# A two-layer RG-LRU and latent-attention trunk on one core: inputs in load order, x and w_ada transposed, modulation by row sums, eight column tiles in the first products

## The chip, the cores and the metric

One core of a Trainium2 chip runs the whole program. A core has five engines that run side by side, each in its own order: TensorE (PE, matmuls; PEld are its weight loads), VectorE (DVE), ScalarE (ACT), GpSimd (POOL) and SyncE (SP), which here issues every transfer; 16 DMA engines move the data. The metric is the device time of one execution in microseconds, as the median of several. Laying out the inputs on the host, ahead of the launch, is not part of it.

## The reference

A residual stream x (512 tokens by 1024) goes through two layers. In each:

```python
mod = (c @ w_ada + b_ada)[:, None, :]                 # c: 1 x 1024, w_ada: 1024 x 6144
sh_m, sc_m, g_m, sh_f, sc_f, g_f = jnp.split(mod, 6, axis=-1)
h = rms_norm(x) * (1 + sc_m) + sh_m
proj = h @ w_in                                       # 1024 x 3520
x_lru, q_down, kv_down, k_rope, gate_a, gate_b = jnp.split(proj, IN_SPLIT_POINTS, axis=-1)
y_a = rg_lru(causal_depthwise_conv(x_lru, conv_w, conv_b), positions, ...)   # 1024 columns
y_b = mla(q_down, kv_down, k_rope, cos, sin, q_norm_g, kv_norm_g, w_uq, w_ukv)  # 256 + 128 + 64
y = jax.nn.sigmoid(gate_a) * y_a + jax.nn.sigmoid(gate_b) * y_b              # 1024 + 1024
x = x + g_m * (y @ w_out)
h = rms_norm(x) * (1 + sc_f) + sh_f
gate, up = jnp.split(h @ w_ffn_in, 2, axis=-1)        # 1024 x 5632
x = x + g_f * ((jax.nn.silu(gate) * up) @ w_ffn_out)  # 2816 x 1024
```

The end is `rms_norm(x, final_norm_g)`. All is float32.

## The kernel before

**Products.** x is held transposed: eight tiles `x[j]` of 128 channels by 512 tokens. Each float32 operand of a product is split into a high and a low part (`split`: ACT rounds the high part to fp32r, DVE subtracts), and a product of 128x128 weights with 128x512 activations is three matmuls (`mm3`): high by high, high by low, low by high. A 128-column tile of `w_in` therefore takes 8 x 3 = 24 matmuls. Its weights come by one transfer into a `raw` buffer of 128x1024 (3 of them), are split into `whi` and `wlo` (3 each) and multiplied into a PSUM bank (8 in all).

**The order of work** is a planner's. The code only records operations; `Recorder.order` then plays them through with estimated durations (`cost`), waits and free buffers, and each engine takes next what has the longest way to the end; PE keeps the order of the code. The words of `SCRIPT` give the code's order in the mixer: `x` conv input, `g` gates, `e` and `w` the recurrence, `r`, `p`, `q`, `s`, `t`, `v` attention, `a`, `b` output gates, `y` merge, `m` one step of background work. Where PE would wait before the first products end, it runs filler matmuls (`fill`, at most `FILL_MAX`).

**The start of layer 0**, to which most of the change belongs:

- x is loaded by tokens: eight `xtok` tiles, whose squares ACT sums (`junk`); PE transposes them by 32 matmuls with `ident`, ACT copies them into `x[j]`. `rsqrt` makes the scale of each token, PE spreads it over the partitions, and it is copied as `rst0` (`rst` in the rows).
- `first_mods` forms the shift and scale of the first norm for one or two tiles j at a time (`FIRST`), as `P`: 8 matmuls per tile and vector, with a block of `w_ada` as weights and the conditioning column spread over 64 columns as the moving side (`pt<-cols,wa`), or as `V`: DVE multiplies and adds eight blocks into `wacc`, and PE sums its partitions (`pt<-ones,wacc`).
- `first_products` then has for each j one column set: `w_first` loads rows j of six column pieces of `w_in` (two of x_lru, two of q_down, kv_down and k_rope), 704 columns in two transfers, and five `mm3` and one `mm2` (k_rope, high and low side by side) add to six banks, 17 matmuls. Eight sets complete the six pieces.

**Modulation vectors later on** (`mod_steps`, 10 of the 12): eight blocks of 128 rows of `w_ada` by 1024 columns are loaded as `graw` (2 buffers); DVE multiplies each by its part of c and adds it to `macc` in two halves of 512; a transposing reduction (`mred`), one matmul with `sel` and four small DVE operations bring the 1024 sums into an 8-column tile. They are the background work: three in the mixer of layer 0, one in the feed-forward part of layer 0 with the six of layer 1.

**Loads.** A tile of 128 columns is read from the row-major weights as 128 partitions x 8 pieces of 512 bytes. Gate weights, `w_uq` and `w_ukv` come in two or three transfers per tile, and small parameters as rows (`rows1`, `rows2`), which PE transposes into columns (`cols1`, `cols2`).

**Small norms** (`small_norm`): squares, sums, `rsqrt`, spreading and scaling of q_down and kv_down, all at one place in the code, right after the first products.

In the rows all operations have the line L525, where the planner issues them; tiles tell them apart.

Of the kernel before, what the change touches and what calls it, by code (L numbers as in the profile page):

```python
# [12 lines left out]
F32 = mybir.dt.float32  # L13
# [4 lines left out]
ALU = mybir.AluOpType  # L18
# [16 lines left out]
OFF_Q = 1024  # L35
OFF_KV = 1280
OFF_KR = 1408
OFF_GA = 1472
OFF_GB = 2496
# [5 lines left out]
C_SEL = 128  # L45
C_MASK = 256
C_FREQ = 768
C_END = 769

R_C = 0  # L50
R_BADA = 8
R_QG = 104
R_KVG = 108
# [4 lines left out]
R_AP = 112  # L58

# [14 lines left out]
GTAG = "graw"  # L74
# [41 lines left out]
DMA_ISSUE = 470.0  # L116
TABLE_LOAD = 1300.0
# [82 lines left out]
class Recorder:  # L200
# [117 lines left out]
    def order(self):  # L318
# [15 lines left out]
        for o in reversed(ops):  # L334
            d = o.dur if o.eng != "SP" else o.bytes / DMA_RATE + DMA_LAT
# [204 lines left out]
def trunk(  # L540
    ctx: ExitStack,
    tc: tile.TileContext,
    x_in, c_in, pos_in, w_ada, b_ada, w_in, conv_w, conv_b,
    lru_wa, lru_ba, lru_wx, lru_bx, lru_ap, qg, kvg,
    w_uq, w_ukv, w_out, w_fi, w_fo, fng, consts, out,
# [66 lines left out]
    def w_cols(src, nk=KD, on_g=False, raws=None):  # L612

        raw = raw_tile()
        DMA.dma_start(raw[:, : nk * P].rearrange("p (k c) -> p k c", c=P), src.rearrange("(k p) c -> p k c", p=P))
        hi, lo = hl_tiles()
        if on_g:
            G.tensor_scalar(hi[:, : nk * P], raw[:, : nk * P], 1.0, 1.0, ALU.mult, ALU.mult)
            V.tensor_tensor(lo[:, : nk * P], raw[:, : nk * P], f(hi[:, : nk * P]), ALU.subtract)
        else:  # L620
            split(hi[:, : nk * P], lo[:, : nk * P], raw[:, : nk * P])
# [4 lines left out]
    def w_krope(l):  # L626

        raw = raw_tile()
        DMA.dma_start(
            raw[:, :512].rearrange("p (k c) -> p k c", c=64),  # L630
            w_in[l, :, OFF_KR : OFF_KR + 64].rearrange("(k p) c -> p k c", p=P),
        )
# [7 lines left out]
    def w_first(l, j, keep):  # L640


        if keep:
            r0, r1 = unit("wf0")[:, :256], unit("wf1")[:, :448]
        else:
            raw = raw_tile()
            r0, r1 = raw[:, :256], raw[:, 256:704]
        js = slice(j * P, (j + 1) * P)
        DMA.dma_start(r0, w_in[l, js, :256])
        DMA.dma_start(r1, w_in[l, js, OFF_Q : OFF_GA])  # L650
        hi, lo = hl_tiles()
# [12 lines left out]
        return parts, hi[:, 640:768], cols + [r1[:, 384:448]]

    def w_lru(l, n0):

        raw = raw_tile()
        for i, src in enumerate((lru_wa, lru_wx)):
            DMA.dma_start(  # L670
                raw[:, i * 512 : (i + 1) * 512].rearrange("p (n c) -> p n c", c=P),
                src[l, n0 : n0 + 4].rearrange("n p c -> p n c"),
            )
        return split_halves(raw, "lw")

    def w_rope(l, g):

        raw = raw_tile()
        for k in range(2):
            DMA.dma_start(  # L680
                raw[:, k * 256 : (k + 1) * 256].rearrange("p (h e) -> p h e", h=4),
                w_uq[l, k * P : (k + 1) * P, 4 * g : 4 * g + 4, NOPE:],
            )
        hi, lo = unit("rwh", F32R), unit("rwl", F32R)
        for k in range(2):
            ks = slice(k * 256, (k + 1) * 256)
            src = raw[:, ks].rearrange("p (h f i) -> p f h i", h=4, f=2)
            dh = hi[:, ks].rearrange("p (f h i) -> p f h i", h=4, f=2)
            dl = lo[:, ks].rearrange("p (f h i) -> p f h i", h=4, f=2)
            A.activation(dh, src, AF.Copy)  # L690
            V.tensor_tensor(dl, src, f(dh), ALU.subtract)
        return hi, lo

    def w_pair(l, p2):

        raw = raw_tile()
        for k in range(2):
            DMA.dma_start(
                raw[:, k * 256 : (k + 1) * 256].rearrange("p (h e) -> p h e", h=2),
                w_uq[l, k * P : (k + 1) * P, 2 * p2 : 2 * p2 + 2, :NOPE],  # L700
            )
        DMA.dma_start(raw[:, 512:].rearrange("p (h e) -> p h e", h=2), w_ukv[l, :, 2 * p2 : 2 * p2 + 2, :])
# [4 lines left out]
    DMA.dma_start(ident, consts[:, :C_SEL])  # L707
    ct = const([P, C_END - C_SEL], "ct")
    sel = ct[:, :P]
    mask = ct[:, C_MASK - C_SEL : C_MASK - C_SEL + 512]  # L710
    freq = ct[:, C_FREQ - C_SEL : C_FREQ - C_SEL + 1]

    rows1, rows2 = unit("rows1"), unit("rows2")
    V.memset(rows1[:, :P], 0.0)
    for rows, r0, n, src in (
        (rows1, R_C, 8, c_in.rearrange("b (j p) -> (b j) p", p=P)),
        (rows1, R_BADA, 96, b_ada.rearrange("l (j p) -> (l j) p", p=P)),
        (rows1, R_QG, 4, qg.rearrange("l (j p) -> (l j) p", p=P)),
        (rows1, R_KVG, 2, kvg),
    ):  # L720
        DMA.dma_start(rows[r0 : r0 + n, :P], src)

    cols1 = const([P, P], "cols1")
    cols2 = const([P, P], "cols2")

    def to_columns(rows, cols):
        ps = psum("pt")
        T.transpose(ps[:, :P], rows[:, :P], ident)
        V.tensor_copy(cols, ps[:, :P])

    to_columns(rows1, cols1)

    ones = const([P, P], "ones")
    V.memset(ones, 1.0)
    epsc = const([P, 1], "epsc")
# [10 lines left out]

    def mod_steps(l, s):

        acc = rec.tile(cp, [P, D], F32, "macc", 1, nm("macc"))
        for k in range(KD):  # L750
            raw = rec.tile(wp, [P, 1024], F32, GTAG, NGRAW if GTAG == "graw" else NRAW, nm("graw"))
            DMA.dma_start(raw, w_ada[l, k * P : (k + 1) * P, s * D : (s + 1) * D])
            ck = cols1[:, R_C + k : R_C + k + 1]
            for h in range(2):
                hs = slice(h * 512, (h + 1) * 512)
                if k == 0:
                    V.tensor_scalar(acc[:, hs], raw[:, hs], ck, None, ALU.mult)
                else:
                    V.scalar_tensor_tensor(acc[:, hs], raw[:, hs], ck, acc[:, hs], ALU.mult, ALU.add)
            yield  # L760
        red = small(32, "mred", 2)
        V.tensor_reduce(red, acc.rearrange("p (b i) -> p b i", i=32), AX.X, ALU.add, apply_transpose=True)
        ps = psum("o")
        T.matmul(ps[:, :32], sel, red, start=True, stop=True)
        m = const([P, 8], f"mod{l}_{s}")
        pv = ps[:, :32].rearrange("p (m r) -> p r m", r=4)
# [914 lines left out]
```

## Time and profile before

| What | Value |
|---|---|
| Median of 3 runs | 1352.01 us (1350.59 to 1353.84) |
| The profiled execution's own time | 1354.54 us |
| Its span, first to last instruction | 1352.5 us |
| DVE, ACT, POOL busy | 987.6, 669.9, 193.4 us (73%, 50%, 14%) |
| Moved by DMA | 175.00 MB, mean 129 GB/s |
| Mean granted clock of TensorE | 0.991 |

The profiled execution is one run of its own, so its time differs a little from the median. Busy time of engines overlaps; a share of the span says how much of the time an engine had an instruction in work, and matmuls are pipelined, so PE's counts overlap among themselves. The granted clock is the share of TensorE's full 2.4 GHz that the throttle gave in a stretch. Times in views are from the span's start.

### The profile page before, as it was taken

The page shows a single profiled execution, that of the slowest core. Times are in us where ns is not written, and L with a number is a line of the kernel's source. Part 1 is how long each engine was busy: PE and PEld are TensorE (multiplying, and loading weights), DVE is VectorE, ACT ScalarE, POOL GpSimd, SP SyncE. Part 2 cuts the span into 40 slices and gives each one's busy share as a digit, 9 for nine tenths or more (in the row PEclk, how much of TensorE's full clock was granted, in tenths as well). Part 3 has the DMA queues.
Part 4 walks back from the last instruction along what each step waited for, and adds up shares of the span by engine and source line. Part 5 has one row for each costly group of instructions (what it writes and reads, how often), then busy time and mean ns, then how long its engine had stood idle before and what let it go on. Part 6 is the DMA issues. An engine that isn't in the chain of part 4 may idle for free.

```text
span 1352.5 us, 18566 instructions
## 1 busy us (share of the span) xinstructions
PE 1331.4 (98%) x6924; PEld 1142.3 (84%) x6924; DVE 987.6 (73%) x1716; ACT 669.9 (50%) x1060; POOL 193.4 (14%) x224
## 2 busy tenths in 40 slices
PE   7999999999999999999999999999999999999997
PEld 7887888888888888888887888888888999999986
DVE  4689799788866556566769976757677877777744
ACT  4386768544523222222346877965364444434422
POOL 0122254411200000000040233422310000000000
PEclk9899999999999999999999999999999999999999
DMA  9544345235655555655534324221333433343321
GB/s 289 176 135 125 106 131 162 94 106 159 192 181 182 185 190 173 205 176 184 186 86 117 102 71 117 66 75 47 94 100 104 119 90 91 104 113 108 98 77 63
DMA packets 251046, 175.00 MB, mean 129 GB/s; under 512 B 12510, under 2 KB 235084, under 8 KB 250956
## 3 DMA queue, kind: packets, MB, share of 16 engines
q1 hardware_dynamic: 250956, 173.82, 43.4%
q8 instruction: 54, 0.88, 0.3%
q14 instruction: 36, 0.29, 0.1%
HBM read 167.50 MB, written 2.10 MB: 125 GB/s over the span
## 4 chain that ended last, share of the span: by engine, by line
PE 87%; DVE 5%; POOL 2%; ACT 2%; DMA 1%; issue 1%; SPq 0%; ACTq 0%; DVEq 0%; POOLq 0%
PE mm L525 77%; PE s L525 4%; PE pt L525 3%; PE o L525 3%; POOL sc L525 1%; POOL w L525 1%; DVE macc L525 1%; DVE xc L525 1%; DVE wlo L525 0%; SPq L525 0%; DVE ri L525 0%; DMA graw<-in_w_ada_dram 0%; DVE xn L525 0%; DVE wacc L525 0%; DMA raw<-in_w_in_dram 0%
## 5 line engine op out<-in xcount | busy, mean ns | idle before, releaser
L525 ACT ACTIVATE whi<-raw 128x1024 fp32r<-128x1024 f32 (+2 forms) x194 | 199.4, 1028 | 417.5 <-PE mm L525 328.8
L525 DVE TENSOR_TENSOR wlo<-raw,whi 128x1024 fp32r<-128x1024 f32 (+2 forms) x193 | 232.3, 1204 | 106.8 <-ACT whi L525 102.7
L525 PE MATMUL mm<-hh,whi 128*128 128x512 f32 x408 | 161.6, 396 | 0.0
L525 PE MATMUL mm<-hl,whi 128*128 128x512 f32 x408 | 160.8, 394 | 0.0
L525 PE MATMUL mm<-hh,wlo 128*128 128x512 f32 x400 | 157.3, 394 | 0.3 <-DVE wlo L525 0.3
L525 PE MATMUL mm<-al,whi 128*128 128x512 f32 (+1 forms) x360 | 139.1, 386 | 0.0
L525 PE MATMUL mm<-ah,whi 128*128 128x512 f32 (+1 forms) x360 | 138.9, 386 | 0.0
L525 PE MATMUL mm<-ah,wlo 128*128 128x512 f32 (+1 forms) x360 | 138.6, 385 | 0.0
L525 PE MATMUL mm<-fh,whi 128*128 128x512 f32 x336 | 130.9, 390 | 0.0
L525 PE MATMUL mm<-fh,wlo 128*128 128x512 f32 x336 | 130.9, 390 | 0.0
L525 PE MATMUL mm<-fl,whi 128*128 128x512 f32 x336 | 130.0, 389 | 0.0
L525 DVE SCALAR_TENSOR_TENSOR macc<-graw,cols,macc 128x512 f32<-128x512 f32 x140 | 101.8, 767 | 17.8 <-DMA graw<-in_w_ada_dram 17.5
L525 PEld LDWEIGHTS mm<-hl,whi 128*128 128x128 f32 x408 | 77.4, 190 | 15.5 <-DVE hl L525 0.5
L525 PEld LDWEIGHTS mm<-hh,whi 128*128 128x128 f32 x408 | 77.3, 189 | 15.5 <-DVE whi L525 0.2
L525 PE MATMUL mm<-xql,wsh 128*128 128x256 f32 x320 | 90.4, 283 | 0.0
L525 PE MATMUL mm<-xqh,wsl 128*128 128x256 f32 x320 | 90.3, 283 | 0.0
L525 PE MATMUL mm<-xqh,wsh 128*128 128x256 f32 x320 | 90.2, 283 | 0.0
L525 PEld LDWEIGHTS mm<-hh,wlo 128*128 128x128 f32 x400 | 75.9, 190 | 16.5 <-DVE wlo L525 1.2
L525 ACT ACT_TABLE_LOAD x60 | 77.0, 1283 | 6.7 <-DVE mx L525 3.2
L525 PEld LDWEIGHTS mm<-ah,wlo 128*128 128x128 f32 x360 | 67.7, 188 | 13.1
L525 PEld LDWEIGHTS mm<-ah,whi 128*128 128x128 f32 x360 | 67.7, 188 | 13.0
L525 PEld LDWEIGHTS mm<-al,whi 128*128 128x128 f32 x360 | 67.7, 188 | 12.7
(299 smaller groups left out, 3026.3 us busy)
## 6 DMA issues: line engine op xcount, KB each, us to landing
raw<-in_w_ffn_in_dram SPq DMA_DIRECT2D x88, 512.0 KB, 4.2
graw<-in_w_ada_dram SPq DMA_DIRECT2D x80, 512.0 KB, 5.0
raw<-in_w_in_dram SPq DMA_DIRECT2D x49, 512.0 KB, 4.2
raw<-in_w_ffn_out_dram SPq DMA_DIRECT2D x32, 448.0 KB, 4.0
wa<-in_w_ada_dram SPq DMA_DIRECT2D x32, 256.0 KB, 5.6
raw<-in_w_out_dram SPq DMA_DIRECT2D x16, 512.0 KB, 4.0
raw<-in_w_ffn_out_dram SPq DMA_DIRECT2D x16, 512.0 KB, 4.1
raw<-in_w_uq_dram SPq DMA_DIRECT2D x24, 128.0 KB, 3.1
```

The lines of the kernel that those rows point to most:

```text
L525: o.call(*(real(v) for v in o.a), **{k: real(v) for k, v in o.k.items()})
```

## The change

All inputs are laid out on the host in the order in which they are loaded: each 128-column tile of `w_in`, `w_out`, `w_ffn_in` and `w_ffn_out` as 128 partitions with one run of 4 KB (3.5 or 4 KB for `w_ffn_out`), gate weights, rope, q and kv weights each as one transfer, the small parameters already as columns (`par1`, `par2`). x and `w_ada` are passed transposed. c is spread over all partitions by a matmul with ones (`cb`).

```diff
+    cb = const([P, D], "cb")
+    for i in range(2):
+        ps, crow, cs = psum("pt"), unit("crow"), slice(i * 512, (i + 1) * 512)
+        DMA.dma_start(crow[:1, :], c_in[:, cs])
+        T.matmul(ps, ones[:1, :], crow[:1, :], start=True, stop=True)
+        A.activation(cb[:, cs], ps, AF.Copy)
...
+    def mod_column(acc, raw, b):
+        V.tensor_tensor_reduce(raw, raw, cb, 1.0, b, ALU.mult, ALU.add, acc)
...
     def mod_steps(l, s):
-        acc = rec.tile(cp, [P, D], F32, "macc", 1, nm("macc"))
-        for k in range(KD):
-            raw = rec.tile(wp, [P, 1024], F32, GTAG, ...
-            DMA.dma_start(raw, w_ada[l, k * P : (k + 1) * P, s * D : (s + 1) * D])
...
+        for j in range(KD):
+            raw = rec.tile(wp, [P, 1024], F32, "graw", NGRAW, nm("graw"))
+            DMA.dma_start(raw, mod_rows(l, s, j))
+            mod_column(m[:, j : j + 1], raw, b[:, j : j + 1])
             yield
...
-    xtok = [[unit("xtok") for _ in range(2)] for _ in range(4)]
...
+    for j in range(KD):
+        DMA.dma_start(x[j], x_in[j * P : (j + 1) * P, :])
+        sq = unit("sq")
+        A.activation(sq, x[j], AF.Square)
         for t in range(4):
+            T.matmul(sums[:, t : t + 1], sq[:, t * P : (t + 1) * P], ones[:, :1],
+                start=j + t == 0, stop=j == KD - 1, skip_group_check=True)
+    rst0 = st0.spread(st0.rstd(sums, FULL, D), FULL, sbuf=True)
...
     def first_products(hh, hl):
+        accs = [psum("mm") for _ in range(NFIRST + 1)]
...
         for j in range(KD):
+            for s, tag, n, b in ((SC_M, "graw", NGRAW, R_BSC), (SH_M, "raw", NRAW, R_BADA)):
+                raw = rec.tile(wp, [P, 1024], F32, tag, n, nm(tag))
+                DMA.dma_start(raw, mod_rows(0, s, j))
+                mod_column(mcol(0, s, j), raw, cols1[:, b + j : b + j + 1])
+            parts, both = w_first(j)
+            make_h(0, SH_M, SC_M, hh, hl, rst0, FULL, [j])
             for i, (wh, wl) in enumerate(parts):
+                mm3(accs[i], wh, wl, hh[j], hl[j], j == 0, j == KD - 1)
...
+            mm2(accs[NFIRST], both, hh[j], hl[j], j == 0, j == KD - 1)
+            if j == TABLES_AT:
+                tables()
...
-            if l == 0 and n < 2:
+            if l == 0 and n < 4:
```

A column set now has seven pieces and k_rope (`NFIRST = 7`, four of x_lru): 960 columns in one transfer, 23 matmuls, and all eight PSUM banks. `make_h` scales x by `rst0` and the scale column in one DVE pass (`ht`), adds the shift on ACT (`hh`) and takes the rest on DVE (`hl`). `first_mods`, its matmuls and `wacc` are gone, and so are `sel`, `mred` and the transposes of x and of the parameter rows. `small_norm` becomes a class with two steps, `d` (squares, sums and scale) and `n` (spreading and the two splits), that `SCRIPT` places; the words of `SCRIPT` are rearranged: layer 0 begins `x0 x4 d0 d1 x1 m1 x5 x2 n0 n1 x3 g0`, where it began `x2 x0 x1 g0 x3 x4` after the small norms; layer 1 begins `d0 d1 m1 m1 m1 n0 n1 x1`. `FILL_MAX` goes from 40 to 70, and the planner counts a transfer as at least 2000 ns when it weighs what is urgent.

## Rows read from the trace of the kernel before

**Rows 1.** Page, busy us with share of the span and instructions by engine; chain's shares by engine.

```profile
PE 1331.4 (98%) x6924; PEld 1142.3 (84%) x6924; DVE 987.6 (73%) x1716; ACT 669.9 (50%) x1060; POOL 193.4 (14%) x224
...
PE 87%; DVE 5%; POOL 2%; ACT 2%; DMA 1%; issue 1%; SPq 0%; ACTq 0%; DVEq 0%; POOLq 0%
```

**Rows 2.** Chain that ended last, saturated stretch: start us, us, what it was.

```profile
351.35 40.30 PE mm L525 x177
```

**Rows 3.** Windows: stretch, length, busy us of PE PEld DVE ACT POOL, clock, DMA, GB/s.

```profile
0.00:22.30 22.30, 18.89 (x141) 17.26 (x142) 5.50 (x25) 14.32 (x30) 0.30 (x5) 0.92 0.93 262
...
0.00:90.00 90.00, 81.28 (x433) 68.91 (x434) 55.37 (x137) 44.45 (x79) 12.79 (x30) 0.91 0.71 208
...
30.00:41.50 11.50, 11.15 (x45) 10.24 (x46) 6.73 (x17) 2.08 (x4) 0.00 (x0) 0.56 1.07 349
...
90.00:150.00 60.00, 57.30 (x257) 47.64 (x257) 55.41 (x89) 42.85 (x65) 15.80 (x13) 0.97 0.51 135
...
150.00:350.00 200.00, 198.66 (x1008) 168.62 (x1007) 170.62 (x335) 123.42 (x214) 68.99 (x73) 1.00 0.42 125
...
350.00:700.00 350.00, 350.00 (x1554) 289.91 (x1553) 229.00 (x310) 107.26 (x133) 16.10 (x22) 1.00 0.56 179
...
700.00:750.00 50.00, 49.57 (x242) 40.75 (x241) 43.96 (x78) 30.25 (x49) 0.00 (x0) 1.00 0.42 113
...
950.00:1303.00 353.00, 353.00 (x2200) 319.75 (x2199) 261.83 (x412) 160.01 (x257) 16.02 (x22) 1.00 0.36 101
```

**Rows 4.** Windows of PE alone, first matmuls on tile hh, then on tile hl.

```profile
0.00:90.00 90.00, 40.13 (x117) 0.91 0.71 208
...
0.00:90.00 90.00, 25.87 (x62) 0.91 0.71 208
```

**Rows 5.** Timeline, 12 to 23 us: start us, duration us, engine, instruction, idle before it.

```profile
12.32 0.63 ACT L525 ACTIVATE junk<-xtok 128x512 f32<-128x512 f32 x1 [0.50 <-DMA xtok<-in_x_dram]
...
14.84 0.30 ACT L525 ACTIVATE hs<-ss,epsc 128x4 f32<-128x4 f32 x1
...
16.58 0.16 DVE L525 SCALAR_TENSOR_TENSOR rs<-nt,rs 128x4 f32<-128x4 f32 x1
...
17.73 0.60 ACT L525 ACTIVATE rst<-pt 128x512 f32<-128x512 f32 x1 [0.17 <-PE pt L525]
...
22.38 0.48 PE L525 MATMUL mm<-hh,whi 128*128 128x512 f32 x1
```

**Rows 6.** Chain that ended last, 30 to 53 us.

```profile
30.98 6.84 PE pt L525 x32
...
48.76 3.53 PE pt L525 x32
```

**Rows 7.** Timeline of PE, 30 us.

```profile
30.09 0.63 PE L525 MATMUL pt<-ones,wacc 128*128 128x64 f32 x4 [3.27 <-DVE wacc L525]
```

**Rows 8.** Groups of DVE, shapes apart: busy us, mean ns of one, idle before.

```profile
L525 DVE TENSOR_TENSOR wlo<-raw,whi 128x896 fp32r<-128x896 f32 x32 | 34.8, 1087 | 17.3 <-ACT whi L525 16.6
...
L525 DVE SCALAR_TENSOR_TENSOR ht<-x,mod,rs 128x512 f32<-128x512 f32 x24 | 17.2, 746 | 3.8 <-ACT rs L525 3.8
...
L525 DVE SCALAR_TENSOR_TENSOR wacc<-wa,cols,wacc 128x256 f32<-128x256 f32 x28 | 12.9, 482 | 0.1
...
L525 DVE CUSTOM_DVE_ANT_0 sc<-s,ct 128x512 f32<-128x512 f32 x16 | 11.0, 685 | 4.2 <-PE s L525 4.2
...
L525 DVE CUSTOM_DVE_ANT_0 sc<-s,ct 128x128 f32<-128x128 f32 x16 | 4.5, 281 | 0.0
...
L525 DVE TENSOR_TENSOR whi<-raw,whi 128x64 fp32r<-128x64 f32 x8 | 1.7, 218 | 0.0
```

**Rows 9.** Tile macc: count, then shortest, median and longest in ns, first and last start.

```profile
L525 DVE SCALAR_TENSOR_TENSOR macc<-graw,cols,macc x140: 733/748/1527, 128.3 to 667.9; 128x512 f32<-128x512 f32 x140
...
L525 DVE TRANSPOSE_TENSOR_REDUCE mred<-macc x10: 1232/1242/1246, 196.7 to 668.7; 128x32 f32<-128x1024 f32 x10
```

**Rows 10.** DMA issues: tile, queue, count, KB each, median us from issue to landing.

```profile
graw<-in_w_ada_dram SPq DMA_DIRECT2D x80, 512.0 KB, 5.0
```

More of the change, by code (lines that the diff above doesn't have):

```diff
@@ L44 @@
 C_ID = 0
[L45 to L53, printed above, removed]
+C_MASK = 128
+C_FREQ = 640
+C_END = 641
+R_BADA = 0
+R_QG = 96
+R_KVG = 100
+R_BSC = 102
+R_END = 110
 R_CW = 0
@@ L58 @@
 R_AP = 112
+NFIRST = 7
 TWO_PI_1 = 6.28125
@@ L628, in w_krope @@
         raw = raw_tile()
[L629 to L632, printed above, removed]
+        DMA.dma_start(raw[:, :512], w_kr[l])
         both, _ = hl_tiles()
@@ L678, in w_rope @@
         raw = raw_tile()
[L679 to L683, printed above, removed]
-        hi, lo = unit("rwh", F32R), unit("rwl", F32R)
[L685 to L691, printed above, removed]
+        DMA.dma_start(raw[:, :512], w_qr[l, g])
+        hi, lo = unit("rwh", F32R), unit("rwl", F32R)
+        split(hi, lo, raw[:, :512])
         return hi, lo
@@ L696, in w_pair @@
         raw = raw_tile()
[L697 to L702, printed above, removed]
+        DMA.dma_start(raw, w_qkv[l, p2])
         return split_halves(raw, "pw")
     ident = const([P, P], "ident")
[L707 to L723, printed above, removed]
-    cols2 = const([P, P], "cols2")
[L726 to L731, printed above, removed]
+    DMA.dma_start(ident, consts[:, :C_MASK])
+    ct = const([P, C_END - C_MASK], "ct")
+    mask = ct[:, :512]
+    freq = ct[:, C_FREQ - C_MASK : C_FREQ - C_MASK + 1]
+    cols1 = const([P, R_END], "cols1")
+    cols2 = const([P, P], "cols2")
+    DMA.dma_start(cols1[:, :R_BSC], par1)
+    V.tensor_scalar(cols1[:, R_BSC : R_BSC + 8], cols1[:, R_BADA + 8 : R_BADA + 16], 1.0, None, ALU.add)
     ones = const([P, P], "ones")
     V.memset(ones, 1.0)
+    cb = const([P, D], "cb")
[4 more added lines that the diff above has]
+        A.activation(cb[:, cs], ps, AF.Copy)
     epsc = const([P, 1], "epsc")
@@ L745, in trunk @@
     mods = {}
-    def mod_steps(l, s):
-        acc = rec.tile(cp, [P, D], F32, "macc", 1, nm("macc"))
-        for k in range(KD):
-            raw = rec.tile(wp, [P, 1024], F32, GTAG, NGRAW if GTAG == "graw" else NRAW, nm("graw"))
-            DMA.dma_start(raw, w_ada[l, k * P : (k + 1) * P, s * D : (s + 1) * D])
[L753 to L759, printed above, removed]
-            yield
[L761 to L766, printed above, removed]
-        for r in range(4):
-            q = slice(32 * r, 32 * r + 32)
-            b = cols1[q, R_BADA + l * 48 + s * 8 : R_BADA + l * 48 + s * 8 + 8]
-            V.scalar_tensor_tensor(m[q, :], pv[q, r, :], 1.0 if s in (SC_M, SC_F) else 0.0, b, ALU.add, ALU.add)
@@ L1468, in layer @@
         drain_bg()
-        if l == 0:
-            for s in (G_M, SC_F, SH_F):
-                if (0, s) not in mods:
-                    for _ in mod_products(0, s):
-                        pass
         gm = const([P, 8], f"gm{l}")
@@ L1491, in layer @@
         na, fast = NAHEAD, NPLAIN[l] + NAHEAD < NF
-        pgu, cgu = ahead.units([w_fi[l, :, c0 + i * P : c0 + (i + 1) * P] for i in range(na) for c0 in (0, D_FF)])
+        pgu, cgu = ahead.units([w_fi[l, c0 + i] for i in range(na) for c0 in (0, NF)])
         if fast:
```

363 lines of the change are left out of this document (125 added, 238 removed).

## Prediction

> **What bounds the kernel now.** I read the busy table and the chain first: PE is busy 98% of the span and 87% of the chain that ended last; DMA is 1% of it [rows 1]. A busy PE may still wait inside or run slowly, so I took its own pace from a saturated stretch: 177 products in 40.30 us, 0.2277 us each [rows 2]. Then the windows by stage [rows 3]. From 350 to 700 and from 950 to 1303 us PE is busy throughout (350.00 and 353.00 us) at granted clock 1.00: nothing that loads faster or takes work off other engines shortens these 703 us. What can shrink lies ahead of 350 us.
>
> There I counted products. Up to 90 us 117 matmuls read `hh` and 62 read `hl` [rows 4]; with 6 gate products that read neither these are 185. At 0.2277 us they are 42.1 us of work in 90 us; 48 us went elsewhere, 22.4 us of it before the first product [rows 5]. From 90 to 150 us PE is busy 57.30 of 60 us, but DVE 55.41 of 60, and up to 350 us 170.62 of 200 [rows 3]. So the mixer of layer 0 has a second engine close to its limit, and that decides how much of an earlier start is kept.
>
> The start: the last token tile is squared at 12.32, the row scale is ready at 16.74, `rst` at 18.33, the first product starts at 22.38 [rows 5]. Between products stand 32 `pt<-cols,wa` matmuls that take 6.84 us at 30.98 and again 3.53 us at 48.76 [rows 6]; ahead of the first PE sat idle 3.27 us for `wacc` [rows 7], and the clock granted from 30 to 41.5 us was 0.56, a mean of the two levels (1.2 and 2.4 GHz). DMA moved 349 GB/s there [rows 3].
>
> **The change part by part.**
>
> *Start.* x comes transposed: 32 transposes and 8 copies go; 8 squares and 32 one-column sum matmuls come, of which 4 wait for the last tile (0.5 us; 32 of the 64-column kind took 3.53 [rows 6]). x is 2.1 MB; at the 262 GB/s of the first window, from 2.4 us after the launch on, it has landed by 10.4. Then a square 0.63, sums 0.5, the row scale 1.9 (14.84 to 16.74), its spreading and copy 1.6 (16.74 to 18.33) [rows 5], one DVE and one ACT pass for `hh` 1.4, and 1 us of hops: 17.4 us. The other path: x and the first column set (two `w_ada` blocks of 512 KB, weights of 480 KB) are 3.6 MB, at the same rate 16.3 us, and 1 us of ACT for the weights: 17.3 too. I take 17.5; bounds 15 (all at 349 GB/s) and 22.4 (nothing gained).
>
> *Column sets.* A set had 17 products, now 7 x 3 + 2 = 23, or 5.24 us of PE; eight sets are 184, 41.9 us. That includes columns 2 and 3 of x, until now 48 products by themselves: no PE work is added. The modulation matmuls go; the 64 of [rows 6] alone cost 10.4 us between products.
> DVE pays for it: each set needs two row sums over 1024. No such width stands in the trace; the same operation (`sc<-s,ct`) takes 281 ns at 128 columns and 685 at 512 [rows 8], 1.05 ns a column, so 1.22 us at 1024, and 0.04 more for reading its accumulator beside the next pass: 1.26 us. Bounds: 1.04 (the 896-wide split, 1.09, less 0.05 that neighbours on DVE overlap) [rows 8] and 3.05 (twice the slowest 512-wide two-input pass, 1527 ns) [rows 9]; I take 1.26, the operation's own slope. With the 896-wide split (1.09), the 64-column rest (0.22) and two 512-wide passes for `ht` and `hl` (0.75 each) [rows 8], each less 0.05, a set is 5.13 us of DVE against 5.24 of PE. DMA: 1.54 MB at 349 GB/s is 4.4 us. Three resources almost level, PE the slowest, and the row sums of the first sets run before `rst` is there. So 17.5 + 41.9 + 1 us for waits: 184 products by 60.5 us, where the old kernel has 185 by 90. By then it has also done 16 sums and 8 spreading transposes for the small norms (3 us of PE) that the new one still owes. Lead: 29.5 - 3 = 26.5 us.
>
> *What is given back.* Of the 55.37 us that DVE worked up to 90 us [rows 3], the old sets' seven groups (from `wacc`, 12.9, to `whi` of 64 columns, 1.7 [rows 8]) are 37, and two splits of x columns, 2.4, go too. The other 16 us (conv, tables, small norms) are pushed behind 60.5 us, into a stretch that was 92% busy. Relief: a modulation vector formed in the mixer takes 16 passes of at most 0.748 and one of 1.24, some 13 us of DVE [rows 9], and will take 8 x 1.26 = 10.1; three of them save 8 us. A product asks DVE for one split in 24 matmuls, so the new order can run products while DVE catches up in the 29 us that it had free from 150 to 350. I take 5 us given back; bounds 0 and 16 (all that is pushed).
>
> *At nothing.* The small norms split in two (`d`, `n`): at the head of layer 1 PE is busy 49.57 of 50 us [rows 3], so there is little idle to fill; up to 3 us if products are slow there for lack of banks. Weights in 4 KB rows instead of 512 B: in the saturated windows PE waits for none, as ACT and DVE split them well ahead; were that cover gone, it would show as PE idle. Seven later modulation vectors: DVE had 121 of 350 us free there. SP: uq, ukv and the gate weights come in one transfer each, and it waits for buffers, not others for it.
>
> **Sum** against the profiled execution of 1354.5 us (2 us around its span of 1352.5; 2.5 above the median of the runs): -26.5 + 5 = -21.5, that is 1333, or 1330 beside the median of 1352.0. The forecast's own range, with a start 3 us off and 0 to 10 us given back: 1322 to 1338.
>
> **The rivals.**
> 1. *The sets starve PE.* Weights and shifts share three `raw` buffers, refilled only when DVE is through; a 512 KB block takes 5.0 us to land beside others [rows 10]. A set holds one buffer for 5 + 1.3 us and another for 5 + 2.3: 13.6 us over three buffers is 4.5 a set, within 5.24, but 2 us of queueing on DVE for each makes it 5.9. Then PE pauses, and the rows show what follows a pause: idle 3.27 us, then a mean clock of 0.56 for 11.5 us [rows 3, 7]. That dip cost 3.3 + 3.3 (32 matmuls at 6.84 instead of 3.53) + 1.8 (the next eight products at half pace, from the end of these to the window's) = 8 us. Two dips: lead 10, 2 given back (DVE is less behind): 1344. For it: the buffers are few. Against: from 30 to 41.5 us DMA was never short of free buffers (share 1.07 [rows 3]). With PE at half pace in all sets (0.455 us a product) they end at 101 us, 11 behind; DVE has no backlog then and keeps its 8 us: about 1357.
> The Trainium skill (TensorE: Matmul & The Clock Gate, section HAM oscillation) says that a wait for the next K-tile's load can drop the clock at every K-tile. The old trace agrees in one place, the 0.56 above; by that rule at every set the time is the 1357 just given.
> 2. *The lead is kept whole*, products covering all of DVE's backlog: -26.5, or -29 with a start at 15; with 2 us from the split norms about 1322.
> 3. *Slower: the row sum costs twice.* One mechanism, on DVE: a 1024-wide two-input pass with accumulator and a column as start value takes 2.5 us instead of 1.26. A set is then 7.6 us of DVE, eight are 61, of which 5 ahead of `rst`: products end at 74, lead 13; the 24 row sums in the mixer put 30 us more on a DVE that had 34 us free from 90 to 350, of which I count 18 as lost, with the 5 above: 13 - 23 = -10, so 1362. It decides from about 2.1 us a row sum on. For it: no row shows the form, and a 512-wide pass has taken 1527 ns [rows 9]. Against: the slope of its own operation.
>
> **How the numbers follow.** Forecast 0.61, starving at some sets 0.16, at all 0.02, lead kept 0.14, slower 0.07. The range 1319 to 1346 leaves out the row sum at twice its price, half pace throughout, the far ends of the second rival and of starving, together under 0.2. About 0.2% (2.7 us) is what a measurement can tell from no change. Faster: the forecast, the lead kept and 0.13 of starving, 0.88; same 0.03, starving at three sets; slower 0.09.
>
> **What would show it.** First product at 15 to 20 us, and 184 of them by 60 to 62; granted clock over 0.95 from 18 to 60; row sums at 1.2 to 1.35 us; DVE over 90% busy from 60 to 120; the saturated stretch that began at 351.35 us [rows 2] begins 17 to 24 us earlier, and its length is as before. Wrong if row sums come over 2 us, if PE pauses of 3 us stand between sets, or if the saturated stretch begins less than 10 us earlier.

## The result, and the profile after

The changed kernel takes 1336.8 us in the median (1336.6 to 1337.1), the kernel before 1351.3 in the same session: a ratio of 0.989, 95% interval 0.987 to 0.991. It is faster, by 14.5 us where 21.5 were forecast. The profiled execution took 1337.1 us with a span of 1335.3 (before: 1352.5), so the spans differ by 17.2. Part of that is the kernel before: its profiled execution (1354.5 us) is 3.2 us above its median here. Beside the later runs its median was 1353.0 to 1353.7, so medians of runs from different sessions are told apart to some 2 us only.

The page, busy us and the chain's shares by engine, against [rows 1]: TensorE still bounds the kernel, with 92% of the chain instead of 87, and VectorE's share fell from 5% to 3.

```profile
PE 1321.1 (99%) x6801; PEld 1131.7 (85%) x6801; DVE 965.5 (72%) x1642; ACT 657.5 (49%) x1037; POOL 206.0 (15%) x224
...
PE 92%; DVE 3%; ACT 2%; POOL 1%; issue 1%; DMA 0%; ACTq 0%; DVEq 0%; POOLq 0%
```

The windows, against [rows 3] (stretch, length, busy us of PE PEld DVE ACT POOL, granted clock, DMA share, GB/s). The stretches from 350 to 700 and from 950 to 1303 us are full in both kernels: TensorE had no pause there to fill, as the prediction had it. From 22.3 to 60 us PE no longer pauses; from 90 to 150 DVE is as full as before.

```profile
0.00:22.30 22.30, 21.05 (x85) 17.20 (x86) 4.64 (x20) 8.65 (x14) 0.30 (x5) 1.00 0.72 262
22.30:60.00 37.70, 37.64 (x178) 30.82 (x176) 35.10 (x59) 14.02 (x19) 1.29 (x5) 1.00 0.74 248
60.00:90.00 30.00, 30.00 (x145) 25.06 (x145) 27.24 (x50) 26.39 (x43) 11.62 (x20) 1.00 0.43 149
90.00:150.00 60.00, 58.35 (x280) 49.11 (x280) 56.59 (x93) 40.30 (x66) 20.35 (x15) 0.97 0.42 128
150.00:350.00 200.00, 196.23 (x967) 165.34 (x966) 168.31 (x323) 120.58 (x209) 76.09 (x72) 0.99 0.41 135
350.00:700.00 350.00, 350.00 (x1554) 289.94 (x1553) 209.81 (x274) 105.84 (x134) 15.75 (x22) 1.00 0.52 175
...
950.00:1303.00 353.00, 353.00 (x2203) 319.70 (x2202) 260.21 (x418) 157.29 (x252) 16.17 (x22) 1.00 0.31 100
```

The start did not come earlier but later. The timeline, against [rows 5]: the squares are done at 10.65 us, but the sums of these squares hold TensorE from 6.57 to 20.38, and the first product starts at 27.71 instead of 22.38.

```profile
6.57 13.81 PE L517 MATMUL o<-ones,sq 128*128 128x1 f32 x64
...
7.30 3.35 ACT L517 ACTIVATE sq<-x 128x512 f32<-128x512 f32 x5
...
20.48 0.26 ACT L517 ACTIVATE hs<-o,eb 128x4 f32<-128x4 f32 x1 [9.84 <-PE o L517]
...
21.38 0.16 DVE L517 SCALAR_TENSOR_TENSOR rs<-nt,rs 128x4 f32<-128x4 f32 x1
...
25.70 0.72 ACT L517 ACTIVATE hh<-ht,mod 128x512 fp32r<-128x512 f32 x1 [0.82 <-DVE ht L517]
...
27.71 1.41 PE L517 MATMUL mm<-hh,whi 128*128 128x512 f32 x5
```

The chain of waits over that stretch (start us, us, what): everything from 6.64 us on is TensorE's own work. 64 narrow matmuls take 13.74 us, 0.2147 apiece; two groups of fillers (matmuls on zeros that keep the engine busy while it would wait) take 3.01 and 3.71 us and stand in the way: the row scale was ready at 21.54 but is spread from 23.39 on, and `hh` was ready at 26.42, 1.3 us ahead of the first product.

```profile
6.64 13.74 PE o L517 x64
20.38 3.01 PE fill L517 x14
23.39 0.85 PE s L517 x4
24.24 3.71 PE fill L517 x27
```

From then on the forecast holds. The eight column sets start at 27.7, 33.5, 38.7, 44.0, 49.2, 54.4, 59.6 and 64.8 us, 5.2 apart, and end at 70.0; a row sum over 1024 columns takes 1.28 to 1.31 us (busy us, mean ns):

```profile
L517 DVE CUSTOM_DVE_ANT_0 graw<-graw,cb,cols 128x1024 f32<-128x1024 f32 x64 | 83.5, 1305 | 9.5 <-DMA graw<-in_w_ada_dram 9.3
...
L517 DVE CUSTOM_DVE_ANT_0 raw<-raw,cb,cols 128x1024 f32<-128x1024 f32 x8 | 10.2, 1278 | 0.9 <-DMA raw<-in_w_ada_dram 0.9
```

The out projection (`yh`), the first step after the mixer, begins at 279.3 us instead of 291.8. The rows of tile `yh`, before and after (ns, then first and last start in us):

```profile
L525 PE MATMUL mm<-yh,whi x128: 387/389/476, 291.8 to 989.8; 128*128 128x512 f32 x128
```

```profile
L517 PE MATMUL mm<-yh,whi x128: 389/389/442, 279.3 to 972.4; 128*128 128x512 f32 x128
```

The saturated stretch of [rows 2] begins at 337.34 us instead of 351.35, and its 1550 products are through in 351.58 us instead of 353.32 (from 351.35 to 704.67). In the chain of the kernel before, seven pieces like the first line stand between them: the two instructions of the `sel` matmul (`o<-mred,ct`), by which each of the seven later modulation vectors was summed. In the changed kernel there are none.

```profile
391.65 0.14 PE o L525 x2
```

```profile
337.34 351.58 PE mm L517 x1550
```

From 60 to 330 us TensorE waits 5.1 us, most of it for VectorE (engine, waited for: total us, times, longest):

```profile
PE mm L517 <- DVE xc L517: 2.2, 1, 2.2
PE s L517 <- DVE kl L517: 1.5, 1, 1.5
PE pt L517 <- POOL sc L517: 1.2, 2, 1.0
```

### The profile page after: what moved, and what is told of

Same layout as the page of the kernel before. It is cut to its first block, busy times and chain, and to the rows that moved or that the text cites. A ratio compares the mean times of both kernels' runs of the same rounds, so it can differ in the third digit from the quotient of the medians.

```text
span 1335.3 us, 18104 instructions
## 1 busy us (share of the span) xinstructions
PE 1321.1 (99%) x6801; PEld 1131.7 (85%) x6801; DVE 965.5 (72%) x1642; ACT 657.5 (49%) x1037; POOL 206.0 (15%) x224
## 2 busy tenths in 40 slices
DMA packets 52555, 174.90 MB, mean 131 GB/s; under 512 B 6642, under 2 KB 6898, under 8 KB 52468
## 4 chain that ended last, share of the span: by engine, by line
PE 92%; DVE 3%; ACT 2%; POOL 1%; issue 1%; DMA 0%; ACTq 0%; DVEq 0%; POOLq 0%
PE mm L517 81%; PE s L517 5%; PE o L517 3%; PE pt L517 2%; PE fill L517 1%; POOL ri L517 0%; POOL sc L517 0%; DVE wlo L517 0%; ACT L517 0%; ACT whi L517 0%; DVE xc L517 0%; DMA raw<-in_w_in_dram 0%; DVE t L517 0%; ACT xc L517 0%; DVE sc L517 0%
## 5 line engine op out<-in xcount | busy, mean ns | idle before, releaser
L517 DVE TENSOR_TENSOR wlo<-raw,whi 128x1024 fp32r<-128x1024 f32 (+1 forms) x191 | 234.6, 1229 | 123.4 <-ACT whi L517 118.7
L517 PE MATMUL mm<-hh,whi 128*128 128x512 f32 x432 | 169.9, 395 | 0.1
L517 PE MATMUL mm<-hl,whi 128*128 128x512 f32 x432 | 169.1, 391 | 0.0
L517 PE MATMUL mm<-hh,wlo 128*128 128x512 f32 x416 | 162.7, 391 | 0.0
L517 PEld LDWEIGHTS mm<-hl,whi 128*128 128x128 f32 x432 | 81.6, 189 | 16.8 <-DVE hl L517 0.5
L517 PEld LDWEIGHTS mm<-hh,whi 128*128 128x128 f32 x432 | 81.6, 189 | 16.8 <-PE fill L517 0.2
L517 DVE CUSTOM_DVE_ANT_0 graw<-graw,cb,cols 128x1024 f32<-128x1024 f32 x64 | 83.5, 1305 | 9.5 <-DMA graw<-in_w_ada_dram 9.3
L517 POOL TENSOR_SCALAR wsa<-raw,mod 128x128 f32<-128x128 f32 x24 | 17.6, 751 | 388.7 <-PE mm L517 338.2
```

The costliest lines, as they stand in the source:

```text
L517: o.call(*(real(v) for v in o.a), **{k: real(v) for k, v in o.k.items()})
```

## The experiments

Theory: the sets do what was forecast; the missing 7 us are lost at the start, in the 64 narrow sum matmuls at 0.21 us. Rivals: the loads of the first set bind there anyway; the parts put at nothing (order, layout) cost something; the gain comes from another part than the row sums. Times are medians, ratios are to the kernel before, with their 95% intervals; e2 was timed once (1344.3 us).

**e1: the squares added on VectorE.** Four sum calls instead of 32.

```
-        sq = unit("sq")
-        A.activation(sq, x[j], AF.Square)
-        for t in range(4):
-            T.matmul(sums[:, t : t + 1], sq[:, t * P : (t + 1) * P], ones[:, :1], ...)
-    rst0 = st0.spread(st0.rstd(sums, FULL, D), FULL, sbuf=True)
+        st0.add(j, x[j], FULL)
+    rst0 = st0.finish(FULL, D, sbuf=True)
```

> The squares of the eight x tiles are added up on VectorE (seven 512-wide passes, an engine that stands idle there) and only four sum calls go to TensorE instead of 32. Theory (the start is set by the 64 narrow sum matmuls at 0.213 us each, 13.8 us in a row): the last square ends at 10.7 us, one more pass 0.7, eight narrow matmuls 1.7, row scale, spreading, rst and hh some 5.5 us: first product at 17.5 to 20 us instead of 27.7, and the lead grows by 8 to 10 us; the mixer's VectorE gives back up to 3 of them, so 1327 to 1331 us. Rival (the first set's loads or their splits bind at the same place): first product stays above 24 us and the time within 3 us of 1337.

Measured: 1329.0 us, ratio 0.982 (0.980 to 0.984), below both kernels and the fastest of all versions here. Two more things differ from the changed kernel: the planner now runs 38 fillers instead of 7 at the very start and has x loaded ahead of c. The timeline of e1:

```profile
5.99 3.88 DVE L517 TENSOR_TENSOR sacc<-sacc,sq 128x512 f32<-128x512 f32 x5 [0.46 <-ACT sq L517]
...
10.01 0.68 DVE L517 TENSOR_TENSOR sacc<-sacc,sq 128x512 f32<-128x512 f32 x1
...
10.85 0.95 PE L517 MATMUL o<-ones,sacc 128*128 128x1 f32 x8
...
17.56 0.96 PE L517 MATMUL mm<-hh,whi 128*128 128x512 f32 x3 [2.36 <-ACT hh L517]
```

The first product starts at 17.56 us, where the prediction had put it (17.5), and the 184 products end at 61.5 (60.5). The loads did not hold up the first product: the rival falls. They show right behind it: of e1's chain from 18 to 42 us, 10.2 us lie on two transfers (4.89 and 5.30). That costs little, as PE is busy 43.22 of the 44 us in which the sets run. Eight narrow matmuls take 0.95 us here, 0.119 apiece, with fillers run right ahead of them.

**e2: wide matmuls between the sums.**

```
             )
+        rec.gate, rec.gate_all = rec.last_pe, True
+        for _ in range(12 if j < KD - 1 else 0):
+            fill_op()
+        rec.gate, rec.gate_all = None, False
```

> The 32 sum calls stay, and behind each of the first seven tiles' four stand 12 filler matmuls of 256 columns (84 in all; the result is the same). Theory (narrow matmuls do the work at full price but leave TensorE at its lower level, 1.2 GHz, from the launch on): once wide ones run between them the narrow ones fall from 0.213 us apiece to 0.107 to 0.13, and the fillers to 0.107. Rival (0.213 us is simply what such a narrow matmul costs, whatever the clock): fillers come down to 0.107 us, narrow ones stay at 0.213. Second rival (the clock can't rise so soon after the launch): both stay at 0.213. Time 1335 to 1350, of no account here.

The timeline of e2 on TensorE:

```profile
12.37 2.72 PE L517 MATMUL fill<-fill_x,fill_w 128*128 128x256 bf16 x12
14.88 1.71 PE L517 MATMUL o<-ones,sq 128*128 128x1 f32 x8
16.45 2.72 PE L517 MATMUL fill<-fill_x,fill_w 128*128 128x256 bf16 x12
18.96 1.15 PE L517 MATMUL o<-ones,sq 128*128 128x1 f32 x8
19.98 1.47 PE L517 MATMUL fill<-fill_x,fill_w 128*128 128x256 bf16 x12
21.29 0.95 PE L517 MATMUL o<-ones,sq 128*128 128x1 f32 x8
```

Both kinds change pace at one moment, near 19 us: eight narrow ones from 1.71 to 0.95 us, twelve fillers from 2.72 to 1.47. So 0.213 us is the narrow matmul's price at the lower level (1.2 GHz) and 0.119 at the higher, and the changed kernel paid the lower one 64 times. The granted-clock column does not show it: it reads 1.00 from 0 to 18 us and from 18 to 30 us of this kernel, on both sides of the change, and 1.00 in the first window of the changed one. So at this start the pace of a known instruction is the surer reading; why the column misses the change is not shown.
The Trainium skill (TensorE: Matmul & The Clock Gate, section What's actually happening) says that the default state is throttled and activity releases it. The pace here agrees, 0.213 us from the launch on and 0.119 after; but 13.7 us of narrow matmuls, in which the profile calls PE busy throughout, did not release it.

**e5: fillers first.** 29 more fillers ahead of everything on TensorE, all 64 sums kept.

```
+    for _ in range(29):
+        fill_op()
     cb = const([P, D], "cb")
```

> The changed kernel with all its 64 narrow sum matmuls, but 29 more wide fillers (256 columns) run first on TensorE, right after the launch, ahead of everything else there. Theory (half of the loss at the start is the clock's lower level, not the number of the sums): the narrow ones run at 0.12 us apiece, the last ends at 16 to 17.5 us instead of 20.4, the fillers behind it cost 0.11 instead of 0.21, first product at 22 to 24 us, 1332 to 1335 us. Rival (TensorE is at its lower level again by the time of the sums, or their number alone counts): first product at 26 us or later, 1336 us or more.

Measured: 1339.2 us, ratio 0.990 (0.988 to 0.992): no gain, the theory missed. First product at 27.51 us. The timeline of TensorE and, below it, the windows of e5:

```profile
8.06 5.71 PE L517 MATMUL o<-ones,sq 128*128 128x1 f32 x40
13.63 0.80 PE L517 MATMUL fill<-fill_x,fill_w 128*128 128x256 bf16 x3
14.22 5.12 PE L517 MATMUL o<-ones,sq 128*128 128x1 f32 x24
```

```profile
10.00:15.00 5.00, 5.00 (x33) 4.88 (x32) 1.61 (x5) 0.98 (x2) 0.00 (x0) 0.64 1.02 407
15.00:20.00 5.00, 5.00 (x25) 4.76 (x25) 0.26 (x3) 0.56 (x2) 0.00 (x0) 0.50 0.44 170
20.00:25.00 5.00, 5.00 (x26) 3.80 (x24) 4.46 (x10) 1.20 (x2) 0.00 (x0) 0.50 0.41 105
```

The first 40 begin at the higher pace (27 of them in 3.17 us, 0.117 apiece); then the granted clock falls to 0.50 in the midst of them, with PE busy 5.00 of 5 us. Their mean is 0.143, and the last 24 pay 0.213 again. A run of narrow matmuls neither raised the clock here nor held it, and fillers ahead of them, of which e1 has 38, bring nothing as long as the 64 follow. So e1's gain comes in the main from the smaller number of sums. (The profiled execution is the fastest of this kernel by 3.6 us, so its later stages are not compared.)

**e7: x by tokens, as before.** Squares summed along rows by ScalarE, 32 transposes and 8 copies, no sums on TensorE; the rest is the changed kernel.

```
-        DMA.dma_start(x[j], x_in[j * P : (j + 1) * P, :])
-        ...
+            DMA.dma_start(xtok[t][i], x_in[0, t * P : (t + 1) * P, i * 512 : (i + 1) * 512])
+            A.activation(unit("junk"), xtok[t][i], AF.Square, accum_out=ss[:, 4 * i + t : 4 * i + t + 1])
+    ...
+            T.transpose(ps[:, t * P : (t + 1) * P], xtok[t][j // 4][:, (j % 4) * P : (j % 4 + 1) * P], ident)
```

> The changed kernel, but x is loaded by tokens as in the kernel before: squares summed along the rows by ScalarE, 32 transposes and 8 copies on the way to the column layout, no sum matmuls. Theory (the transposed x, with its sums on TensorE, was itself a loss of time at the start): rst near 18.3 us as in the kernel before, first product at 20 to 22 us instead of 27.7, 1330 to 1333 us, faster than the changed kernel. Rival (the transposes and copies queue up with the first set's splits on ScalarE): first product at 24 to 27 us, 1334 to 1337. Second rival (x by columns is a gain as such): 1338 or more.

Measured: 1333.8 us, ratio 0.986 (0.985 to 0.988), first product at 21.49 us, 6.2 earlier than in the changed kernel. By the medians 3 us faster; the interval touches that of the changed kernel's second run (e9), so the time alone barely tells them apart. What the start shows is plain: by itself, x by columns with its sums on TensorE was a loss; with e1's sums the start is 4 us earlier than with tokens (17.56 against 21.49).

**e3: six column tiles a set instead of eight.**

```
-NFIRST = 7
+NFIRST = 5
-            if l == 0 and n < 4:
+            if l == 0 and n < 2:
```

> The eight column sets of the first products take six column tiles, as in the kernel before, instead of eight: 17 products a set, and columns 2 and 3 of x come later as 48 products by themselves. Theory (VectorE needs about 4.9 us a set whatever the number of tiles, so a set of 17 products, 3.9 us of TensorE, is bound by VectorE): 136 products by 66 to 67 us where the changed kernel has 184 by 70; lead smaller by 7.5 us, of which the mixer makes good a few: 1340 to 1345 us. Rival A (the backlog of VectorE in the mixer swallows the difference): 1335 to 1339. Rival B (the pauses in every set bring the clock down, granted clock near 0.5 to 0.7 from 28 to 66 us): above 1348.

Measured: 1339.2 us, ratio 0.990 (0.988 to 0.991), which cannot be told from the changed kernel's 0.989: the theory missed, rival A is nearer. The out projection begins at 279.9 us (279.3 in the changed kernel). A set took 4.2 us (33.9 us for eight), not 4.9; several row sums had run before the first set. Two more tiles are the same products done sooner, under VectorE's passes; they are worth 2 us or nothing, which these runs cannot tell.

**e6: the first modulation on TensorE.** Built on e1, with six tiles; the `w_ada` blocks come in 512-byte pieces.

```
-                mod_column(mcol(0, s, j), raw, cols1[:, b + j : b + j + 1])
+                for k in range(KD):
+                    T.matmul(pm[:, :64], raw[:, k * P : (k + 1) * P], ccol[:, k : k + 1].to_broadcast([P, 64]), ...)
+                V.tensor_tensor(mcol(0, s, j), pm[:, :1], cols1[:, b + j : b + j + 1], ALU.add)
```

> Built on e1 (squares added on VectorE, first product at 17.6 us) with six column tiles a set, and in the first sets the scale and shift columns come from TensorE, 16 matmuls of 64 columns a set (128 in all), in place of VectorE's 16 row sums. Theory (the row sums' worth is these matmuls: 128 at 0.11 us stand between the products): 14 us of TensorE more, of which the sets' own pauses (0.4 us each) hide 2 to 4; with 2 us for the two tiles moved 1339 to 1344 us against 1329 of e1. Rival A (VectorE, freed of 2.5 us a set, gives the time back in the mixer): 1330 to 1336. Rival B (w_ada in 512-byte pieces starves the sets and the clock falls): above 1347.

Measured: 1357.7 us, ratio 1.004 (1.002 to 1.005): 29 us behind e1, far beyond the expectation. The expectation counted calls: 128. The tile's view shows twice as many instructions:

```profile
L517 PE MATMUL pt<-ccol,graw x128: 217/275/421, 13.5 to 73.2; 128*128 128x64 f32 x128
```

and as many on `raw`: a call on f32 operands is two. 256 at 0.11 (3.53 for 32 [rows 6]) would be 28 us. 48 of them run before the first product, at a granted clock of 0.55 between 10 and 25 us, and it starts at 27.24 instead of 17.56. From 27 to 83 us, while the sets run, the clock reads 1.00, so rival B is out. So without the row sums there is no gain (1.004, against 0.982 in e1). What they brought against the kernel before, e6 does not show: that kernel ran half as many such instructions, 128 on `wa` from 13.7 to 52.0 us, with VectorE doing the rest.

**e8 and e11: VectorE's load in the mixer.** e8 leaves the mixer's 24 row sums out, e11 does them twice.

```
-            mod_column(m[:, j : j + 1], raw, b[:, j : j + 1])
+            if l == 0:
+                V.tensor_tensor(m[:, j : j + 1], raw[:, :1], b[:, j : j + 1], ALU.add)
...
```

```
             mod_column(m[:, j : j + 1], raw, b[:, j : j + 1])
+            if l == 0:
+                V.tensor_tensor_reduce(raw, raw, cb, 1.0, zero, ALU.mult, ALU.add, small(1, "twice", 2))
...
```

> Leaves out the 24 row sums of the three modulation vectors that are formed in layer 0's mixer (each of their columns is set by a one-element add; their loads stay, and the order on TensorE is the same): 31 us less work for VectorE between 70 and 280 us, and a result that is not the reference's. Theory (VectorE near its limit gives back part of the lead): the out projection begins 3 to 5 us earlier than at 279.3, 1332 to 1334 us. Rival (the products hide VectorE's backlog, and the given-back time is TensorE's own small waits or late loads): within 1 us, 1336 to 1338.

> Each of the 24 row sums of the mixer's three modulation vectors is done twice (the second into a column that nobody reads): 33 us more for VectorE between 70 and 280 us. Theory as the prediction's third rival sized it (some 30 us more on VectorE, 18 of them lost): the out projection begins 12 to 20 us later than at 279.3 and the time is 1349 to 1357 us. Rival (the same slope as in e8, where 31 us less brought 5): 1340 to 1345. Second rival (hidden by products that need little of VectorE): within 2 us of 1337.

e8: 1331.9 us, ratio 0.984 (0.983 to 0.986), 5 us under the changed kernel; the out projection begins at 274.1 us instead of 279.3 (277.1 in e9). All that TensorE still waits for from 60 to 330 us in e8:

```profile
PE s L517 <- DVE kl L517: 1.5, 1, 1.5
PE mm L517 <- ACT ri L517: 0.4, 1, 0.4
```

The waits for `xc` and `sc` are gone: the row sums in the mixer cost TensorE 3 us (against e9) to 5 us (against the changed kernel's first profile). Of the 2.2 us between these two executions of one kernel 0.7 lie at the start (27.71 and 27.04); the rest goes with the clock: both wait 2.1 to 2.2 us for `xc`, but the granted clock behind the wait is 0.91 in the first and 1.00 in e9 (windows of PE alone, the changed kernel, then e9):

```profile
170.00:190.00 20.00, 17.84 (x80) 0.91 0.47 154
```

```profile
170.00:190.00 20.00, 17.90 (x85) 1.00 0.43 146
```

e11: 1364.5 us, ratio 1.009 (1.007 to 1.010), 27.7 us behind the changed kernel for 33 us of work: the out projection begins at 293.5, and TensorE then waits 8.3 us more for VectorE's sum of squares, as the last row sums stand in front of it. The windows of e11:

```profile
150.00:280.00 130.00, 115.02 (x563) 96.31 (x562) 113.03 (x233) 79.44 (x147) 54.93 (x46) 0.95 0.35 114
280.00:350.00 70.00, 62.92 (x300) 52.84 (x298) 66.66 (x109) 27.33 (x44) 28.24 (x26) 0.99 0.39 128
```

31 us less bring 5, 33 us more cost 28: the changed kernel stands at the edge of what VectorE can bear. The out projection is as late as the theory of e11 had it (14 us against 12 to 20), but the time is 7 us above its range: the 8.3 us behind the out projection were not thought of.

**e4 and e10: the parts put at nothing.** e4 loads the product weights row-major in 512-byte pieces, e10 has the old order of steps with whole small norms ahead of it.

```
 e4  -        DMA.dma_start(raw[:, : nk * P], src)
     +        DMA.dma_start(raw[:, : nk * P].rearrange("p (k c) -> p k c", c=P), src.rearrange("(k p) c -> p k c", p=P))
 e10 -SCRIPT = ('x0 x4 d0 d1 x1 m1 x5 x2 n0 n1 x3 ...
     +SCRIPT = ('d0 n0 d1 n1 m1 x2 x0 x1 g0 x3 x4 g1 ...
```

> All weights of the in, out and FFN products lie row-major again and are loaded in 512-byte pieces, as in the kernel before; the rest is the changed kernel. Theory (loads are hidden everywhere but at the start, which these weights do not touch): weight loads land 0.5 to 1 us later in the median, time within 2 us of 1336.8. Rival (the mixer's loads are late without the 4 KB rows): 1340 to 1350, with TensorE waits on whi or wlo from 70 to 350 us.

> The changed kernel with the order of steps that the kernel before had in both layers; the small norms are done whole ahead of it (sums, spreading and scaling at once), as before. Theory (order and split norms were put at nothing, up to 3 us): within 3 us of the changed kernel, 1335 to 1340. Rival (the new order is what keeps TensorE fed in the mixer while VectorE is behind): 1341 or more, with idle TensorE at the norms near 70 us.

e4: 1336.9 us (ratio 0.988, 0.987 to 0.990), though 226763 packets were moved instead of 52555 and `w_in` blocks land in 4.2 us instead of 3.5. e10: 1337.1 us (0.988, 0.987 to 0.990); TensorE idles at the norms (27.93 of 30 us from 60 to 90) and makes it good later. Both are worth nothing that these runs can tell, as costed. The other new layouts (gate, q and kv weights in one transfer each, the small parameters as columns) have no run of their own.

**e9: the changed kernel again.**

> The changed kernel itself, run beside the next three on one chip, so that small differences can be read: 1336 to 1338 us, first product at 27 to 28 us.

1336.8 us (1334.4 to 1337.0), ratio 0.988 (0.986 to 0.989); first product at 27.04 us, out projection at 277.1.

**e12: the mixer's row sums off VectorE.** On e1; GpSimd multiplies, ScalarE sums.

```
-            mod_column(m[:, j : j + 1], raw, b[:, j : j + 1])
+            if l == 0:
+                for i in range(2):
+                    hs = slice(i * 512, (i + 1) * 512)
+                    G.tensor_tensor(raw[:, hs], raw[:, hs], cb[:, hs], ALU.mult)
...
+                A.activation(raw, raw, AF.Copy, accum_out=rsum)
+                V.tensor_tensor(m[:, j : j + 1], rsum, b[:, j : j + 1], ALU.add)
...
```

> Built on e1: the products of the mixer's 24 row sums are formed by GpSimd (two 512-wide passes each, 1.2 to 1.5 us a pass in the rows of the changed kernel, 58 to 72 us in all) and summed by ScalarE (some 1.1 us each), so VectorE has 31 us less. Theory (VectorE's lateness costs e1 what TensorE waits for in the mixer, xc 2.2, sc 1.1, mx 0.4 us): 1325 to 1327 us, 2 to 4 below e1. Rival (GpSimd's two-input passes hold up VectorE or the gates' own GpSimd steps): 1329 us or more.

Measured: 1341.3 us, ratio 0.992 (0.990 to 0.993), 12 us behind e1; the rival holds. VectorE's groups from 60 to 280 us, first in e1, then in e12:

```profile
L517 DVE TENSOR_TENSOR wlo<-raw,whi 128x1024 fp32r<-128x1024 f32 x22 | 29.8, 1354 | 7.1 <-ACT whi L517 6.5 <-PE pt L517 0.5
...
L517 DVE TENSOR_TENSOR_SCAN ri<-a,ri 128x512 f32<-128x512 f32 x8 | 10.7, 1337 | 0.6 <-POOL ri L517 0.6
```

```profile
L517 DVE TENSOR_TENSOR wlo<-raw,whi 128x1024 fp32r<-128x1024 f32 x22 | 34.5, 1567 | 8.7 <-ACT whi L517 4.4 <-PE pt L517 4.2
L517 DVE TENSOR_TENSOR_SCAN ri<-a,ri 128x512 f32<-128x512 f32 x8 | 13.7, 1714 | 1.7 <-POOL ri L517 1.7
```

The same 1024-wide split takes 1567 ns instead of 1354, the scan 1714 instead of 1337: VectorE is busy for 194.2 us from 60 to 280 us in both, though 17 row sums of e1 (24.1 us) are gone from that stretch in e12: its other passes took up what it was spared. Whether the kernel lost its 12 us by these passes or by GpSimd's own later steps, the two parts of the rival, no run separates. The Trainium skill (SBUF — State Buffer, section Summary: rules for kernel authors) says that of a VectorE pass with two SBUF inputs and a GpSimd one that reads SBUF, the second to issue blocks until the first is done. The longer passes agree with it; no run here shows a single block.

## Why the prediction was right in kind and 7 us short

*What bounds, and where to win*: right in the main. 14.0 of the 17.2 us arise before the saturated stretch, and the one from 950 us on is as long as before. But the first got 1.7 us shorter, as matmuls were taken out of TensorE itself, and 1.6 us more were won at the head of layer 1.

*The start*: this step failed, by the size of one term. It was put at 17.5 us, bounds 15 to 22.4; it is 27.7. The term that was mis-sized is "32 one-column sum matmuls come, of which 4 wait for the last tile (0.5 us ...)". From the last square (10.65) to the last sum (20.38) it was 9.7 us. Two readings were wrong. A call is two instructions, so a tile's four sums are eight. And the price, 3.53 us for 32 [rows 6], was taken from a stretch with wide products around it; the other row of the same group, 6.84 for 32 (0.214 apiece), was the right one here. At 1.7 us a tile the sums fell behind the squares of the last five tiles, which came 0.67 us apart. The prediction has no term for the fillers, which cost 1.7 us ahead of the spreading (14 at 0.215, the lower pace too) and 1.3 ahead of the first product. These 12 us were eased by some 2 in the other terms: the row scale took 1.2 us instead of 1.9. e1 takes the 56 instructions away and lands at 17.56 us, so the sum of the other terms was right.

*The sets*: right. 41.9 us and 1 for waits were forecast, 42.3 were measured; 1.26 us a row sum, against 1.28 to 1.31. The pace of 5.2 us a set leaves nothing for the first rival: no dip at any set (PE busy 42.24 of 42.30 us).

*The lead*: forecast 26.5 us, measured 90 - 70 - 3 = 17; e1, with the start as forecast, has 90 - 61.5 - 3 = 25.5.

*Given back*: forecast 5 us, bounds 0 and 16. The out projection begins 12.5 us earlier than before, so 4.5 were given back, or about 3 by e9 (14.7 earlier). The size is right, and e8 shows that VectorE's load costs time there. The reasoning, by the backlog that is pushed behind the sets, is not borne out: in e1, with a lead of 25.5, the out projection begins at 267.2, 24.6 earlier, and only 1 us is given back. e1 waits as long for `xc` and `sc` (2.2 and 1.1 us), but 0.3 us for `kl` instead of 1.5, and its granted clock is 1.00 where the changed kernel has 0.91 (from 110 to 130 and from 170 to 190 us). Why the same load cost less there stays open.

*After the mixer*, up to the end, another 4.7 us were won (12.5 to 17.2), which no term of the sum had. About 1.5 came by the start of the saturated stretch (14.0), 1.7 within it, of which the seven `sel` matmuls are 1.0, and 1.6 at the head of layer 1: from 704.67 to 785.98 us before, from 688.92 to 768.66 after, where waits of TensorE for VectorE's row scales (0.4 us) and for GpSimd's `sc` (0.6) are gone. The order is not it (e10 is as fast); what took these waits away stays open. This was luck: the lead came out 9.5 us short, and without these 4.7 the time would lie at some 1341 us, outside the forecast's own range of 1322 to 1338.

*At nothing*: right for layout and order, by e4 and e10. Of the seven later modulation vectors only VectorE's side was weighed; their `sel` matmuls on TensorE were worth the 1.0 us above.

*The third rival*, a row sum at twice its price, did not occur, but its working was too kind: e11 puts 33 us on VectorE and loses 28, where 18 of 30 were counted.

Of the marks named, the row sums and VectorE over 90% busy (27.24 of 30 us from 60 on, 56.59 of 60 from 90 on) came true. The granted clock did by its column alone: from 18 us to the end of the first fillers at 23.4 the pace was the lower one. The first product, the 184th and the saturated stretch 17 to 24 us earlier (it is 14.0) did not come true because of the start; in e1 the first two do, and that stretch begins 25.8 us earlier, at 325.56. The stretch is 1.7 us shorter, not as before.

## What to carry to other kernels

Price a short matmul by the pace that TensorE has at that place, and count its instructions, not its calls: the same one cost 0.213 us after the launch and 0.119 beside wide products. A reduction that feeds the first product belongs on an engine that idles there; here seven VectorE passes replaced 56 matmuls and brought 8 us more. When an instruction goes, look whether it stood in a saturated stretch of the engine that bounds: there its time is won in full, as with the seven `sel` matmuls. And an engine that is not the bound may still stand at its edge: 31 us less on VectorE brought 5, 33 us more cost 28.

## What the runs showed of the hardware that was not expected

- TensorE can be busy by the profile and lose its clock: in e5 the granted clock fell to 0.50 during a run of one-column f32 matmuls (5.00 of 5 us busy), in e6 it was 0.55 over 15 us in which it ran 64-column ones, fillers and short pauses.
- The granted-clock column read 1.00 from the launch on while the pace was about half (in e2, 0.213 us for a matmul that took 0.119 later in the same execution).
- With 48 two-input passes put on GpSimd, VectorE's took 16 and 28% longer in the two groups shown (1354 to 1567 ns, 1337 to 1714 ns).
- One wait of 2.1 to 2.2 us of TensorE was followed by a lower granted clock in one execution (0.91 over the 20 us around it) and not in another of the same kernel (1.00).
